# A hybrid decoder layer on one core: the gates of the recurrence made in two groups of two chunks

## The chip, the cores and the metric

The kernel runs on one core of a Trainium2 chip. The metric is the device time of one execution in microseconds (us). The median of the runs is given, with the lowest and the highest. One further execution was taken with the hardware profiler, and all views below are of that one.

## The reference

One layer for 512 tokens of width 1024: a half-step SwiGLU feed-forward part, a mixer, and a second half-step SwiGLU part, each between two RMS norms. Only the mixer matters here. It projects its input to four things: the recurrence's input (4 chunks of 128 channels), the recurrence's output gate, the queries of 8 heads (again 4 chunks of 128 rows), and the keys and values of 2 heads.

```
def block_diag(x, w, b):                      # 8 blocks of 64 x 64
    xh = x.reshape(bsz, s, LRU_BLOCKS, LRU_BLOCK)
    y = jnp.einsum("bshi,hij->bshj", xh, w).reshape(bsz, s, D_LRU)
    return y + b

def rg_lru(x_in, ...):
    xc = causal_depthwise_conv(x_in, conv_w, conv_b)
    r = sigmoid(block_diag(xc, w_rg, b_rg))
    i = sigmoid(block_diag(xc, w_ig, b_ig))
    log_a = LRU_C * r * log_sigmoid(lam)
    a, mult = exp(log_a), sqrt(-expm1(2.0 * log_a))
    u = mult * (i * xc)
    ...                                       # h[t] = a[t] * h[t-1] + u[t]

def hybrid_mixer(h, ...):
    ...
    y_lru = rg_lru(x_lru, ...) * gelu(gate_lru)
    y_attn = sliding_window_sink_attention(q, k, v, sinks)
    y = concatenate([rms_norm(y_lru, g_lru_out), rms_norm(y_attn, g_attn_out)])
    return y @ w_o
```

Attention runs in blocks of 128 queries over a band of two blocks of keys.

## The kernel before

The activations lie with channels on the partitions and the 512 tokens along the row, so a chunk is a tile of 128 x 512. Every float32 product is made of three matmuls on a high and a low part (`mm3`, L505 to L507): high times high, high times low, low times high. A product of a full chunk has 8 steps of 3, so 24 matmuls.

The order of instructions on each engine is the order of the calls in the source (the schedule is manual). What can still shift is only when each instruction starts: it waits for its operands and, where it is the first to write a tile, for all users of the old tile whose buffer it takes over. Four pools of buffers matter: `bank` gives one of 8 PSUM banks, `t2k` one of 38 SBUF tiles of 2 KB a partition, `wt` one of 8 SBUF working tiles (tag "w"), and `home` is one wide tile that holds the queries and keys for the first block. When the program is built, a new `wt` tile is put in a buffer that an earlier one has given up.

The stretch in question, in the order of the calls:

- `conv(0, xps)` makes the convolution of chunks 0 and 1: ACT starts each (L1443), and DVE adds three taps to each (L1447). `split_xc(ci)` then rounds a chunk to its high part on ACT (`xch`, L1473) and takes the low part on POOL (`xcl`, L1474).
- `in_product("pk")`, `in_product("pv")` and, in the loop over j, `in_product(f"pq{j}")` are the products for keys, values and the four query chunks on TensorE (PE). Each `W.take` in them also splits weights that come later: the high part on ACT (`whi`, L209), the low part on DVE or POOL (`wlo`, L214).
- `conv(2, xps)` makes the convolution of chunks 2 and 3, ahead of the loop.
- In round j of the loop: the query product `pq{j}`; `split_xc(j + 1)`; `lru_gates(j)`; and `in_parts`, which handles the query: DVE scales it into the working tile `qT{j}` (L1427) and copies the first 128 tokens to `home` (L1487), ACT rounds it (L1493), DVE takes the low part (L1494). In round 0 four transposes of the values follow (`vt`, L1513), which DVE copies out (L1515).
- `lru_gates(ci)` makes the two gates of one chunk. The blocks are 64 x 64, and the two halves of the partitions (`SIDE`) are multiplied at the same time in two halves of the array: 3 pairs of matmuls (L1455) into the banks `rg` and `ig`. ACT takes two sigmoids (L1457, L1459). They hold one half of each gate, so two transfers from SP's queue (L1458, L1460) put the halves of the input gate together in the working tile `ig`, POOL multiplies it into the chunk (L1462, written `xc<-ig,xc` in the views), and POOL's queue moves the other half (L1463).
- After the loop ACT loads the table for the exponential (L481), and the attention starts: the first scores `cur` (L1597) need all four query copies in `home`; DVE masks them and takes the maximum (L1616, L1617, L1631), ACT takes the exponentials (L1642), PE transposes them (`pt`, L1652) and ACT copies them out (L1654). Between these PE works at the products of the output gate (`gt`).

Of the kernel before, what the change touches and what calls it, by code (L numbers as in the profile page):

```python
# [11 lines left out]
AF = mybir.ActivationFunctionType  # L12
# [11 lines left out]
KC = C // P  # L24
# [97 lines left out]
def tile_layer(ctx: ExitStack, tc: tile.TileContext, out: bass.AP, **ins: bass.AP):  # L122
    nc = tc.nc
    pe, dve, act, pool, sync = nc.tensor, nc.vector, nc.scalar, nc.gpsimd, nc.sync
# [14 lines left out]
    SIDE = [slice(0, HD), slice(HD, P)]  # L139

    def bank(name):
        return psum.tile([P, T], F32, tag="bank", name=name)

    def t2k(name, dt=F32):
        return big.tile([P, T], dt, tag="t2k", name=name, bufs=NT2K)
# [3 lines left out]
    def fours(name, dt):  # L149
        t = big.tile([P, NB * T], dt, tag="z", name=name, bufs=2)  # L150
        return [t[:, i * T:(i + 1) * T] for i in range(NB)]
# [10 lines left out]
    def wt(name, w=T, dt=F32):  # L162
        return tmp.tile([P, w], dt, tag="w", name=name, bufs=NW)
# [5 lines left out]
    def load_raw(srcs, nk, w, name):  # L169
        raw = wpool.tile([P, nk * w], F32, tag="raw", name=f"raw_{name}", bufs=NRAW).rearrange("p (k c) -> p k c", k=nk)  # L170
        o = 0
        for src in srcs:
            n = src.shape[1]
            sync.dma_start(raw[:, :, o:o + n], src.rearrange("(k p) c -> p k c", p=P))
            o += n
        return raw
# [215 lines left out]
    for g, (f0, f1) in enumerate(GROUPS2):  # L392
        if g == 0:
            for f in range(f0, f1, 2):
                add_gate_up(w2, f, "b")
            r = W.raw(lambda f=f0: load_raw([ins["ffn2_w_down"][0, f * P:(f + 2) * P, :]], 2, D, f"bd{f}"))
# [40 lines left out]
    for i in range(2):  # L437
        load_x(0, i)
        for o in (0, F):
            r = first_raw[o, i] = t2k(f"first{o}{i}").rearrange("p (k c) -> p k c", k=4)  # L440
# [9 lines left out]
    for name, n in ROWS:  # L450
        if name in ("b_rg", "b_ig"):

            j = name == "b_ig"
# [33 lines left out]
    def colrange(name):  # L487
        lo, n = col_of[name]
        return cols[:, lo:lo + n]

    def col(name, i):
        return colrange(name)[:, i:i + 1]
# [16 lines left out]
    def product(w, xs, sl=ALL, name="", hooks=()):  # L509
        ps = bank(name)  # L510
        hooks = dict(hooks)
        for k, x in enumerate(xs):
            if k in hooks:
                hooks[k]()
            mm3(ps[:, sl], w, k, [t[:, sl] for t in x], k == 0, k == len(xs) - 1)
        return ps
# [683 lines left out]
    banks = [bank(f"a_first{i}") for i in range(4)]  # L1200
# [96 lines left out]
    gw, home = {}, []  # L1297
# [125 lines left out]
    def in_product(name, hooks=(), ahead=AHEAD):  # L1423
        return product(W.take(ahead), mx.xs, name=name, hooks=hooks)

    def scaled(t, b):
        dve.tensor_mul(t, b, R)  # L1427
        return t

    xcs, th, rs_, us_ = [], [], [], []  # L1430
# [15 lines left out]
                ci = c0 + j  # L1446
                dve.scalar_tensor_tensor(xcs[ci], xps[ci][:, 1 + w:1 + w + T], col("conv_w", w * KC + ci), xcs[ci], op0=ALU.mult, op1=ALU.add)  # L1447

    def lru_gates(ci):

        banks = bank(f"rg{ci}"), bank(f"ig{ci}")
        (hi, lo), (xh, xl) = gw["both"], xc_parts[ci]
        for i, (w, x) in enumerate(((hi, xh), (hi, xl), (lo, xh))):
            for ps, half in zip(banks, SIDE):
                pe.matmul(ps, w[half, ci, :], x[half, :], start=i == 0, stop=i == 2)  # L1455
        r, other, ig = t2k(f"r{ci}"), wt(f"other{ci}"), wt(f"ig{ci}")
        act.activation(r, banks[0], AF.Sigmoid, bias=col("b_rg", ci))  # L1457
        sync.dma_start(ig[SIDE[0], :], r[SIDE[1], :])  # L1458
        act.activation(other, banks[1], AF.Sigmoid, bias=col("b_ig", ci))  # L1459
        sync.dma_start(ig[SIDE[1], :], other[SIDE[0], :])  # L1460
        u = xcs[ci]
        pool.tensor_mul(u, ig, u)  # L1462
        pool.dma_start(r[SIDE[1], :], other[SIDE[1], :])  # L1463
        t = t2k(f"th{ci}")
        rs_.append(r)
        us_.append(u)
        th.append(t)

    xc_parts = {}

    def split_xc(ci):
        xh, xl = wt(f"xch{ci}", T, F32R), wt(f"xcl{ci}", T, F32R)
        act.copy(xh, xcs[ci])  # L1473
        pool.tensor_sub(xl, xcs[ci], xh.bitcast(F32))  # L1474
        xc_parts[ci] = xh, xl
# [8 lines left out]
    def in_parts(b, first, name, low=dve):  # L1484

        x = scaled(wt(name), b)
        dve.tensor_copy(first, x[:, :P])  # L1487
        if name == "qT3":
            spare.extend(fours("attn", F32R))
            xh, xl = spare.pop(), spare.pop()  # L1490
        else:
            xh, xl = t2k(f"{name}h", F32R), t2k(f"{name}l", F32R)
        act.copy(xh, x)  # L1493
        low.tensor_sub(xl, x, xh.bitcast(F32))  # L1494
        return xh, xl

    conv(0, xps)
    split_xc(0)
    kT = in_parts(pk, k0, "kT", pool)
    pv = in_product("pv")  # L1500
    vT = scaled(wt("vT"), pv)
    conv(2, xps)
    qT = []
    for j in range(4):
        b = in_product(f"pq{j}")
        if j < KC - 1:
            split_xc(j + 1)
        lru_gates(j)
        qT.append(in_parts(b, q0[:, j * P:(j + 1) * P], f"qT{j}", deferred if j == 3 else dve))
        if j == 0:  # L1510
            vt = bank("vt")
            for b in range(NB):
                pe.transpose(vt[:, b * P:(b + 1) * P], vT[:, b * P:(b + 1) * P], ident)  # L1513
            v = home[0][:, P + 2 * T:P + 2 * T + 8 * (HD + 1)]
            dve.tensor_copy(v.rearrange("p (h d) -> p h d", d=HD + 1)[:, :, :HD], vt.rearrange("p (h d) -> p h d", d=HD))  # L1515
# [285 lines left out]
    ws, banks = [], []  # L1801
# [31 lines left out]
    banks = boundary(res, late, ysp, None, n2, "m")  # L1833
# [192 lines left out]
```

## Time and profile before

| | us |
|---|---|
| median of 3 runs | 844.31 |
| lowest, highest | 844.1, 844.48 |
| the profiled execution | 844.61 |
| its span, first to last instruction | 842.9 |
| PE busy in the span | 834.0 (99%) |
| DVE busy | 729.9 (87%) |
| ACT busy | 520.7 (62%) |
| POOL busy | 184.6 (22%) |

The profiled execution took 1.7 us more than its span, and 0.3 us more than the median. A busy PE is only one that has a matmul under way; matmuls overlap, and how tightly they follow each other is read from their starts. In the views a row of the timeline gives start, duration, engine, line, operation, tiles (out<-in) and count, and in brackets how long the engine had stood idle before it and what ended that. Buffer numbers are left out, so the four queries are all called `qT` and the four chunks `xc`.

### The profile page before, as it was taken

The numbers are of one execution on the slowest core, as the hardware profiler recorded it, in microseconds if no ns is written. First come the engines' busy times: TensorE is split into PE (matmuls) and PEld (weight loads), VectorE is DVE, ScalarE is ACT, GpSimd is POOL, SyncE is SP. The second block draws the span as 40 slices with busy tenths as digits, with TensorE's granted clock in tenths as the row PEclk, the third lists the DMA queues.
The fourth block names the chain that finished last, engine by engine and source line by source line (L and its number), as shares of the span: only waits on it lengthen the run. The fifth ranks groups of instructions, "written<-read, shape, count | busy, mean of one in ns | idle before, by whom it ended". The sixth has DMA issues, their size and how long they took to land.

```text
span 842.9 us, 12574 instructions
## 1 busy us (share of the span) xinstructions
PE 834.0 (99%) x4568; PEld 722.1 (86%) x4568; DVE 729.9 (87%) x1031; ACT 520.7 (62%) x837; POOL 184.6 (22%) x197
## 2 busy tenths in 40 slices
PE   9999999999999999999999999999999999999997
PEld 8988888988988998997788899888888888888886
DVE  4978999998979865889789589799998998998996
ACT  6746856666666654456796456436657767666562
POOL 2023000140320333334521055112004114032001
PEclk9999999999999999999999999999999999999999
DMA  7249419397595799222511131169539939769742
GB/s 251 77 132 350 155 54 323 81 247 257 131 248 184 170 268 335 77 80 90 157 51 51 50 107 45 51 127 276 192 105 230 316 96 250 256 147 254 304 145 101
DMA packets 123614, 143.74 MB, mean 171 GB/s; under 512 B 23896, under 2 KB 81568, under 8 KB 123040
## 3 DMA queue, kind: packets, MB, share of 16 engines
q1 hardware_dynamic: 109232, 111.86, 41.6%
q0 software_dynamic: 14176, 30.94, 17.0%
q8 instruction: 36, 0.59, 0.3%
q14 instruction: 26, 0.21, 0.1%
q10 hardware_dynamic: 144, 0.13, 0.0%
HBM read 100.45 MB, written 40.89 MB: 168 GB/s over the span
## 4 chain that ended last, share of the span: by engine, by line
PE 93%; DVE 3%; ACT 2%; DMA 1%; issue 0%; POOL 0%; DVEq 0%; POOLq 0%; ACTq 0%
PE ab L955 10%; PE aa L955 10%; PE da L955 5%; PE db L955 5%; PE yaa L1346 3%; PE bb L955 3%; PE ba L955 3%; PE yda L1346 2%; PE ya L505 2%; PE ya L506 2%; PE ya L507 2%; PE a_first L1205 1%; PE aa L885 1%; PE yab L1867 1%; PE yab L1866 1%; PE yab L1865 1%
## 5 line engine op out<-in xcount | busy, mean ns | idle before, releaser
L1115 POOL DMA_DIRECT2D yp_a<-stage x42 | 36.8, 1065 | 181.0 <-ACT stage L1112 163.5
L1115 POOL DMA_DIRECT2D yp_b<-stage x42 | 36.3, 1053 | 144.0 <-ACT stage L1112 121.4
L505 PE MATMUL ya<-hha,whi_ad 128*128 128x512 f32 x62 | 24.1, 389 | 0.0
L506 PE MATMUL ya<-hla,whi_ad 128*128 128x512 f32 x62 | 24.1, 389 | 0.0
L507 PE MATMUL ya<-hha,wlo_ad 128*128 128x512 f32 x62 | 24.1, 389 | 0.0
L688 POOL TENSOR_TENSOR acca_r<-acca_r,sq_r 128x512 f32<-128x512 f32 x6 | 8.1, 1357 | 63.7 <-ACT sq_r L536 63.7
L1984 POOL TENSOR_TENSOR last<-yp,grow 128x512 f32<-128x512 f32 x3 | 3.9, 1293 | 58.3 <-DVE yp L1974 58.3
L524 PE MATMUL an<-xh_mx,whi_xl 128*128 128x256 f32 x64 | 15.8, 287 | 0.0
L525 PE MATMUL an<-xh_mx,wlo_xl 128*128 128x256 f32 x64 | 15.5, 283 | 0.0
L1981 ACT ACTIVATE ysq<-yp 128x512 f32<-128x512 f32 (+1 forms) x8 | 4.9, 607 | 15.9 <-DVE yp L1974 15.9
L505 PE MATMUL gt<-xh_mx,whi_gt 128*128 128x512 f32 x32 | 14.2, 444 | 0.0
L507 PEld LDWEIGHTS ya<-hha,wlo_ad 128*128 128x128 f32 x62 | 11.6, 188 | 2.4
L505 PEld LDWEIGHTS ya<-hha,whi_ad 128*128 128x128 f32 x62 | 11.6, 188 | 2.4
L506 PEld LDWEIGHTS ya<-hla,whi_ad 128*128 128x128 f32 x62 | 11.6, 188 | 2.4
L1112 ACT COPY stage<-yab 128x512 f32<-128x512 f32 x12 | 6.5, 604 | 11.3 <-DMA yp_b<-stage 11.3
L505 PE MATMUL pq<-xh_mx,whi_q 128*128 128x512 f32 x32 | 12.8, 400 | 0.0
L536 ACT ACTIVATE sq_r<-yp_a 128x256 f32<-128x256 f32 (+1 forms) x10 | 5.0, 502 | 12.3 <-DVE yp_a L678 5.9
L505 PE MATMUL pub<-xh_f,whi_bu 128*128 128x512 f32 x32 | 12.6, 395 | 0.0
L507 PE MATMUL gt<-xh_mx,wlo_gt 128*128 128x512 f32 x32 | 12.6, 394 | 0.0
L505 PE MATMUL pgb<-xh_f,whi_bg 128*128 128x512 f32 x32 | 12.6, 393 | 0.0
L506 PE MATMUL gt<-xl_mx,whi_gt 128*128 128x512 f32 x32 | 12.5, 392 | 0.0
L506 PE MATMUL pq<-xl_mx,whi_q 128*128 128x512 f32 x32 | 12.5, 390 | 0.0
(2017 smaller groups left out, 3501.7 us busy)
## 6 DMA issues: line engine op xcount, KB each, us to landing
yp_a<-stage POOLq DMA_DIRECT2D x50, 256.0 KB, 8.8
yp_b<-stage POOLq DMA_DIRECT2D x50, 256.0 KB, 9.1
h_a<-za SPq DMA_DIRECT2D x16, 256.0 KB
hxa<-h_a SPq DMA_DIRECT2D x16, 256.0 KB
h_b<-zb SPq DMA_DIRECT2D x16, 256.0 KB
hxb<-h_b SPq DMA_DIRECT2D x16, 256.0 KB
xn<-in_x SPq DMA_DIRECT2D x8, 256.0 KB
xT_hbm<-xT POOLq DMA_DIRECT2D x2, 1024.0 KB, 9.3
```

The costliest lines, as they stand in the source:

```text
L505: pe.matmul(ps, hi[:, k, :], xh, start=start, stop=False)
L506: pe.matmul(ps, hi[:, k, :], xl, start=False, stop=False)
L507: pe.matmul(ps, lo[:, k, :], xh, start=False, stop=stop)
L524: pe.matmul(ps[:, sl], hi[:, k, :], xh, start=k == 0, stop=False)
L525: pe.matmul(ps[:, sl], lo[:, k, :], xh, start=False, stop=False)
L885: pe.matmul(o, w[:, k, js], x, start=first and i + j + k == 0, stop=k == 3 and i == 2, skip_group_check=True)
L955: pe.matmul(b[tb], x[:, blk], w[:, k, :], start=first and q + k + j == 0, stop=q + k == 2 and j == 2, skip_group_check=True)
L1115: pool.dma_start(o, st.rearrange("p (a b) -> p a b", a=2) if len(o.shape) == 3 else st, accum_op=ALU.add)
L1205: pe.matmul(banks[j][:, HALF[0]], ws[j][part][:, k, :], n1.xs[k][xpart][:, HALF[0]], start=k == 0 and part == xpart, stop=stop and k == KD ...
L1346: pe.matmul(o, a[:, k, ms], x[:, js], start=first and i + k + m % 2 == 0, stop=k == 1 and i == 2, skip_group_check=True)
L1865: pe.matmul(banks[i], hh[:, js], hi[:, k, :], start=first and k == 0, stop=False, skip_group_check=True)
L1866: pe.matmul(banks[i], hh[:, js], lo[:, k, :], start=False, stop=False, skip_group_check=True)
```

## The change

`lru_gates` now takes a tuple of chunks and a function to be called between its two parts. First it issues the matmuls of all its chunks, step by step over the three parts and within a step chunk by chunk; then the sigmoids and SP's transfers of all its chunks; then `between()`; and then POOL's products and transfers. It is called twice: behind query product 0 for chunks 0 and 1, and behind query product 2 for chunks 2 and 3. No gates stand behind products 1 and 3 any more. Chunk 1 is split ahead of the value product; chunks 2 and 3 are split in `between()` of the first group, that is, on ACT behind four sigmoids and on POOL ahead of the first two products `xc<-ig,xc`. The number of instructions of each kind is unchanged.

```
-    def lru_gates(ci):
-        banks = bank(f"rg{ci}"), bank(f"ig{ci}")
-        (hi, lo), (xh, xl) = gw["both"], xc_parts[ci]
-        for i, (w, x) in enumerate(((hi, xh), (hi, xl), (lo, xh))):
-            for ps, half in zip(banks, SIDE):
-                pe.matmul(ps, w[half, ci, :], x[half, :], start=i == 0, stop=i == 2)
...
+    def lru_gates(cs, between=lambda: None):
+        banks = {ci: (bank(f"rg{ci}"), bank(f"ig{ci}")) for ci in cs}
+        hi, lo = gw["both"]
+        for i in range(3):
+            for ci in cs:
+                xh, xl = xc_parts[ci]
+                w, x = ((hi, xh), (hi, xl), (lo, xh))[i]
+                for ps, half in zip(banks[ci], SIDE):
+                    pe.matmul(ps, w[half, ci, :], x[half, :], start=i == 0, stop=i == 2)
+        gates = {}
+        for ci in cs:
+            r, other, ig = gates[ci] = t2k(f"r{ci}"), wt(f"other{ci}"), wt(f"ig{ci}")
+            act.activation(r, banks[ci][0], AF.Sigmoid, bias=col("b_rg", ci))
+            sync.dma_start(ig[SIDE[0], :], r[SIDE[1], :])
+            act.activation(other, banks[ci][1], AF.Sigmoid, bias=col("b_ig", ci))
+            sync.dma_start(ig[SIDE[1], :], other[SIDE[0], :])
+        between()
+        for ci in cs:
+            r, other, ig = gates[ci]
+            u = xcs[ci]
+            pool.tensor_mul(u, ig, u)
+            pool.dma_start(r[SIDE[1], :], other[SIDE[1], :])
...
     kT = in_parts(pk, k0, "kT", pool)
+    split_xc(1)
     pv = in_product("pv")
...
         b = in_product(f"pq{j}")
-        if j < KC - 1:
-            split_xc(j + 1)
-        lru_gates(j)
+        if j == 0:
+            lru_gates((0, 1), lambda: (split_xc(2), split_xc(3)))
+        if j == 2:
+            lru_gates((2, 3))
         qT.append(in_parts(b, q0[:, j * P:(j + 1) * P], f"qT{j}", deferred if j == 3 else dve))
```

The buffers that the working tiles take over move with it. In the built program of before, the write of `qT0` waits for no product `xc<-ig,xc`, and the write of `qT2` waits for that of chunk 1, whose `ig` buffer it takes. In the built program of after, the write of `qT0` takes the buffer of `ig` of chunk 0 and waits for POOL's product of chunk 0; the write of `qT1` waits for that of chunk 1; the writes of `qT2` and `qT3` wait for none. The bank of query product 3 is that of query product 0 in both.

More of the change, by code (lines that the diff above doesn't have):

```diff
@@ L1447, in conv @@
                 dve.scalar_tensor_tensor(xcs[ci], xps[ci][:, 1 + w:1 + w + T], col("conv_w", w * KC + ci), xcs[ci], op0=ALU.mult, op1=ALU.add)
-    def lru_gates(ci):
-        banks = bank(f"rg{ci}"), bank(f"ig{ci}")
-        (hi, lo), (xh, xl) = gw["both"], xc_parts[ci]
-        for i, (w, x) in enumerate(((hi, xh), (hi, xl), (lo, xh))):
-            for ps, half in zip(banks, SIDE):
[L1455 to L1467, printed above, removed]
+    def lru_gates(cs, between=lambda: None):
[20 more added lines that the diff above has]
+            pool.dma_start(r[SIDE[1], :], other[SIDE[1], :])
+            rs_.append(r)
+            us_.append(u)
+            th.append(t2k(f"th{ci}"))
     xc_parts = {}
```

## The prediction

> **What bounds the kernel now.** I read the page first, then the waits by engine, then the chain that ended last, and then the timelines of the mixer's start, engine by engine.
>
> ```profile
> span 842.9 us, 12574 instructions
> PE 834.0 (99%) x4568; PEld 722.1 (86%) x4568; DVE 729.9 (87%) x1031; ACT 520.7 (62%) x837; POOL 184.6 (22%) x197
> ...
> PE atp L1763 <- DVE yn L1704: 0.6, 1, 0.6
> ...
> 409.23 0.89 PE cur L1597 x16
> ...
> 413.08 0.52 ACT sc L1642 x2
> ...
> 455.88 1.64 PE atp L1763 x13
> ```
>
> TensorE is busy for 99% of the span, and in the mixer it waits once, 0.6 us for DVE at `atp`. From 413 to 456 the chain runs through ACT and DVE instead, and its start is PE's own place: ACT copies out what PE has just transposed. So PE and that chain move together: what delays PE at the first scores, `cur`, comes out at the end whole, and what it gains there comes out too. At most the 0.6 us at `atp` could still give way. The question is when `cur` is done. The rows of PE around it:
>
> ```profile
> 394.85 0.39 PE L507 MATMUL pq<-xh_mx,wlo_q 128*128 128x512 f32 x1
> 395.16 0.50 PE L1455 MATMUL rg<-xch,gates 64*128 64x512 f32 x1
> ...
> 396.05 0.50 PE L505 MATMUL pq<-xh_mx,whi_q 128*128 128x512 f32 x1
> 396.39 0.39 PE L506 MATMUL pq<-xl_mx,whi_q 128*128 128x512 f32 x1
> 396.62 0.40 PE L507 MATMUL pq<-xh_mx,wlo_q 128*128 128x512 f32 x1
> ...
> 407.95 0.39 PE L507 MATMUL pq<-xh_mx,wlo_q 128*128 128x512 f32 x1
> 408.27 0.50 PE L1455 MATMUL rg<-xch,gates 64*128 64x512 f32 x1
> ...
> 409.07 1.05 PE L1597 MATMUL cur<-home 64*128 64x128 f32 x16
> ...
> 413.60 0.60 PE L1652 MATMUL pt<-ident,sc 128*128 128x128 f32 x4
> ```
>
> **The change on PE.** Full matmuls follow each other at 0.23 us (396.39 to 396.62). From the last matmul of product 1 (394.85) to the second of product 2 (396.39) are 1.54 us, where two steps of 0.23 would be 0.46: a group of gates costs 1.08 us. Its three pairs are worth 0.69; the other 0.39 is the change from full rows to half rows and back. Before, there are four such changes (the last group and `cur` share one); after, there are three: two double groups, and `cur` alone. Up to the end of product 3, PE gains 3 pairs (0.69) ahead of product 1, loses a whole group (1.08) ahead of product 2, and gains 0.69 ahead of product 3: its last matmul goes from 407.95 to 408.25. `cur` follows 0.32 later (as 408.27 follows 407.95), at 408.57 instead of 409.07; with the 0.11 us that the first matmul after a change costs, PE by itself is 0.39 us earlier. That is all there is to win there.
>
> `cur` goes through the four query chunks in turn; the fourth starts after three quarters of the chain's 0.89 us, at 409.07 + 0.67 = 409.74 before, and could start at 409.3 after. It needs the copy of `qT3`.
>
> **The change on DVE and POOL.** Here is the price.
>
> ```profile
> 389.11 6.04 DVE L1447 SCALAR_TENSOR_TENSOR xc<-xp,cols,xc 128x512 f32<-128x512 f32 x6 [0.51 <-ACT xc L1443]
> ...
> 396.21 0.68 DVE L1427 TENSOR_TENSOR qT<-pq,R_mx 128x512 f32<-128x512 f32 x1
> ...
> 400.01 0.68 DVE L1427 TENSOR_TENSOR qT<-pq,R_mx 128x512 f32<-128x512 f32 x1
> ...
> 404.39 0.69 DVE L1427 TENSOR_TENSOR qT<-pq,R_mx 128x512 f32<-128x512 f32 x1 [1.18 <-POOL xc L1462]
> 405.11 1.14 DVE L1487 COPY home<-qT 128x128 f32<-128x128 f32 x1
> 406.18 0.68 DVE L1494 TENSOR_TENSOR qT2l<-qT,qT2h 128x512 fp32r<-128x512 f32 x1
> 406.78 1.21 DVE L214 TENSOR_TENSOR wlo_gt<-raw_gt__4100,whi_gt 128x1024 fp32r<-128x1024 f32 x1
> 408.38 0.69 DVE L1427 TENSOR_TENSOR qT<-pq,R_mx 128x512 f32<-128x512 f32 x1 [0.39 <-PE pq L507]
> 409.11 0.23 DVE L1487 COPY home<-qT 128x128 f32<-128x128 f32 x1
> ```
>
> ```profile
> 396.38 1.29 POOL L1462 TENSOR_TENSOR xc<-ig,xc 128x512 f32<-128x512 f32 x1 [3.77 <-DMA ig<-other]
> 397.61 0.56 POOL L1463 DMA_DIRECT2D r<-other  x1
> ...
> 404.86 1.30 POOL L1474 TENSOR_TENSOR xcl<-xc,xch 128x512 fp32r<-128x512 f32 x1
> 406.86 2.28 POOL L1462 TENSOR_TENSOR xc<-ig,xc 128x512 f32<-128x512 f32 x1 [0.70 <-DMA ig<-other]
> ```
>
> ```profile
> 392.55 0.69 ACT L1457 ACTIVATE r<-rg,cols 128x512 f32<-128x512 f32 x1
> 393.14 0.68 ACT L1459 ACTIVATE other<-ig,cols 128x512 f32<-128x512 f32 x1
> ...
> 400.73 0.62 ACT L1493 CAST qT1h<-qT 128x512 fp32r<-128x512 f32 x1 [0.55 <-DVE qT L1427]
> 401.25 1.05 ACT L209 CAST whi_gt<-raw_gt__4100 128x1024 fp32r<-128x1024 f32 x1
> ...
> 411.06 1.28 ACT L481 ACT_TABLE_LOAD   x1
> ...
> 412.47 1.13 ACT L1642 ACTIVATE sc<-cur,nm 128x128 f32<-128x128 f32 x4
> 414.28 0.59 ACT L1654 COPY pa<-pt 128x512 f32<-128x512 f32 x1 [0.68 <-issue]
> ```
>
> Two things show. First, DVE and POOL hold each other up when both work from SBUF alone: the copy at 405.11 takes 1.14 us and ends with POOL's split (404.86 + 1.30), while its twin at 409.11 takes 0.23; POOL's product at 406.86 takes 2.28 instead of 1.29 and ends 1.15 us after DVE's weight split (406.78 + 1.21). Reading a query from PSUM (408.38) is not held. Second, a query may wait for a buffer: at 404.39 DVE waited 1.18 us for POOL's product of chunk 1.
>
> After, `qT0` is the one that waits, for POOL's product of chunk 0, and that product now stands behind both splits of chunks 2 and 3, which need the second convolution:
>
> - The convolution ends at 395.15 now (389.11 + 6.04). ACT's rounding of chunk 1 (0.62) goes ahead of the weights, which delays what follows on ACT and DVE by up to 0.6; POOL's split of chunk 1 no longer falls into the convolution, which saves up to 1.0 of waiting. I take 395.45, between 394.9 and 396.0.
> - ACT rounds both chunks behind four sigmoids, which end at 395.0 (from 392.55, 0.59 apart): chunk 2 at 395.6, chunk 3 at 396.2. By then DVE has started a weight split (1.21) at the end of the convolution, to 396.6. POOL then does two splits and the product, 3 x 1.29 less small overlaps: 400.3. If POOL gets in ahead of DVE, the same four pieces fill the same time.
> - So `qT0` starts at 400.35 instead of 396.21, and everything behind it on DVE's queue with it: the rest of query 0, the copy of `vt`, a weight split, `qT1`.
> - Round 0 took 3.80 (396.21 to 400.01). Its copy to `home` now meets POOL's second product: 400.3 + 0.56 of issuing + 1.29 = 402.1, 0.3 later in the round than the first product's end was. `qT1` at 404.4. Its own buffer is free by then.
> - Round 1 took 3.20 without its wait (400.01 to 404.39 less 1.18): `qT2` at 407.55.
>
> ACT holds round 2:
>
> - ACT rounds `qT1` 0.72 after its start (400.01, 400.73), at 405.1; the weights' high part from 405.65 to 406.7; then four sigmoids in a row at 0.59 (392.55, 393.14), to 409.0; then it rounds `qT2`, to 409.6. PE has filled their banks by 403, but in ACT's queue they stand behind `qT1`.
> - DVE's low part of `qT2` starts at 409.6; from there to the next query are 1.73 (406.18 to the end of 406.78 + 1.21, less 0.08 of overlap): `qT3` at 411.35, its copy from 412.07.
> - POOL's product of chunk 2 comes 2.56 us after the sigmoid that ends at 407.9 (393.14 + 0.68 to 396.38), at 410.45, waits for the weight split and runs from 411.35 to 412.65. The copy ends with it, at 412.7.
>
> The fourth quarter of `cur` starts at 412.75 instead of 409.74: **+3.0 us**. Product 3 takes the bank of product 0, which DVE has read by 401.0, and PE reaches it 23 steps ahead of 408.25, at 403: no wait.
>
> The sum's ends: with the convolution at 394.9 and no turn lost to POOL at the last copy (0.4), +2.0; with POOL's products of chunks 2 and 3 both ahead of DVE's last weight split and copy (another 1.29 less 0.1), +4.2. The 0.6 us at `atp` would lower the first end to +1.4 if it went, which I don't expect: the exponentials of the first block come at 414.8 (the table, 1.28, is loaded by 414.0), are done by 415.95, and PE reaches the transposes at 413.60 + 3.0 = 416.6. So from there all is as before, 3.0 later.
>
> On SP's queue the second load of the output weights stood between gate transfers and now stands behind all of them, at about 409.6.
>
> ```profile
> 404.62 0.54 SPq L174 DMA_DIRECT2D raw_wo__4325<-in_w_o  x1
> ...
> 427.01 1.03 ACT L209 CAST whi_wo<-raw_wo__4325 128x1024 fp32r<-128x1024 f32 x1
> ```
>
> Its first reader comes 22.4 us after its issue, which leaves more than 17: nothing. The sigmoids of chunk 3 are earlier than before, and their readers are not waiting.
>
> The profiled execution took 844.61 us for 842.9 of span; I expect 847.6 and 845.9, and 844.31 + 3.0 = 847.3 for the median. A change of 0.2% is 1.7 us, about what a measurement of this kernel can tell from none.
>
> **The rivals.**
>
> *POOL and DVE run freely (845.7).* If they don't exclude each other and the stretched rows have another cause, the convolution and the copies are quicker. `qT0` then waits only for ACT and POOL: chunk 2 rounded at 395.6, two splits and a product, 399.5. Without held copies round 0 takes 3.7 and round 1 3.1, so `qT1` comes at 403.2; ACT's row of work behind it (0.7 + 0.5 + 0.95 + 4 x 0.59 + 0.62) puts the low part of `qT2` at 408.4, `qT3` at 410.1 and its copy at 411.1: +1.4, or +0.8 if the wait at `atp` goes. That is not slower by what can be measured. It decides at a last copy by 411.4. For it: DVE stood idle at two queries above, 1.57 us together. Against it: 1.14 and 0.23 for the same copy, and POOL's 2.28. A last copy by 409.7, which would be no loss at all, would need `qT0` by 398, and the four sigmoids and two splits ahead of it don't allow that. Chance 0.10.
>
> *POOL takes the turns (848.5).* POOL's products for chunks 2 and 3 fall just where `qT3` is scaled and copied; if they win, +4.2. For it: at 406.86 POOL stood only 0.08 behind DVE. Chance 0.15.
>
> *The clock falls (849.0).* PE stands still from about 409.3 to 412.75, 3.4 us in one piece.
>
> ```profile
> 382.00:410.00 28.00, 28.00 (x144) 21.51 (x142) 24.30 (x30) 18.34 (x26) 16.87 (x12) 1.00 0.38 113
> ```
>
> Here PE never rested (28.00 busy of 28.00 us) at a granted clock of 1.00, so no row shows what a rest does. If matmuls ran at twice their pitch of 0.23 for as long again, half of 3.4 would be lost: +3.0 + 1.7. [...] Chance 0.07.
>
> **How the numbers follow.** The forecast has 0.66: 0.63 from +1.7 to +3.6, and 0.03 under that. POOL's turns have 0.15, the clock 0.07, the free run 0.10, and 0.02 stay for a gain by waits that I don't see. Slower is 0.63 + 0.15 + 0.07 = 0.85, same 0.03 + 0.10 = 0.13, faster 0.02. The range goes from 845.6 (+1.3), just under the free run, to 848.9 (+4.6), the end of the clock's case; outside lie the 0.02 and about half of the free run, of the short end and of the clock, 0.12 in all. Leaving out the free run whole would leave out 0.2, but its bound hangs on ACT's row, which is the surest of the terms, so I keep it in.
>
> **What would show it.** In the profile of after: DVE's first `qT` at about 400 instead of 396.2 with POOL's `xc` as its releaser; POOL with two splits and two products in a row from 396; ACT with four sigmoids in a row from about 406.6, ahead of the rounding of `qT2`; the fourth `qT` after 411; a wait of PE at `cur` for DVE's copy `home`, 3 us or more, where none was; and from `pt` on the rows of before, 3 us later, with 0.6 left at `atp`. The prediction is wrong if `qT0` comes before 399, if PE doesn't wait at `cur`, or if that wait is made good before `atp`.

## The result, and the profile after

| | us |
|---|---|
| before, median of 6 runs | 844.17 (843.98 to 844.48) |
| after, median of 6 runs | 849.85 (848.6 to 851.09) |
| ratio, with its 95% interval | 1.0062 (1.0052 to 1.0073) |
| the profiled execution of after | 850.22, span 848.5 |

The kernel is 5.7 us slower. The forecast was 847.3 us, with a range up to 848.9: the direction was right, the size was not. The changed kernel was run five times more, beside the experiments: 849.04 us (848.33 to 850.58) against 844.33, ratio 1.006 (1.0048 to 1.0073).

First the waits of TensorE (total, times, longest):

```profile
PE cur L1606 <- DVE home L1494: 3.0, 1, 3.0
...
PE atp L1772 <- DVE yn L1713: 0.6, 1, 0.6
```

The wait at `cur` is new; the 0.6 us at `atp` is as before. The timelines of DVE, POOL and ACT in the stretch that the prediction went through:

```profile
400.49 0.69 DVE L1427 TENSOR_TENSOR qT<-pq,R_mx 128x512 f32<-128x512 f32 x1 [3.67 <-POOL xc L1470]
...
404.63 0.68 DVE L1427 TENSOR_TENSOR qT<-pq,R_mx 128x512 f32<-128x512 f32 x1
...
407.73 0.69 DVE L1427 TENSOR_TENSOR qT<-pq,R_mx 128x512 f32<-128x512 f32 x1
...
409.76 0.69 DVE L1501 TENSOR_TENSOR qT2l<-qT,qT2h 128x512 fp32r<-128x512 f32 x1 [1.08 <-ACT qT2h L1500]
...
411.51 0.68 DVE L1427 TENSOR_TENSOR qT<-pq,R_mx 128x512 f32<-128x512 f32 x1
412.23 0.57 DVE L1494 COPY home<-qT 128x128 f32<-128x128 f32 x1
```

```profile
395.81 3.40 POOL L1481 TENSOR_TENSOR xcl<-xc,xch 128x512 fp32r<-128x512 f32 x2 [3.99 <-ACT xch L1480]
399.18 1.28 POOL L1470 TENSOR_TENSOR xc<-ig,xc 128x512 f32<-128x512 f32 x1
...
410.62 2.11 POOL L1470 TENSOR_TENSOR xc<-ig,xc 128x512 f32<-128x512 f32 x1 [7.87 <-DMA ig<-other]
```

```profile
406.81 0.68 ACT L1462 ACTIVATE r<-rg,cols 128x512 f32<-128x512 f32 x1
...
409.10 0.63 ACT L1500 CAST qT2h<-qT 128x512 fp32r<-128x512 f32 x1
```

Both holds are there: the first query waits 3.67 us for POOL's product behind two splits, and the rounding of `qT2` stands behind four sigmoids. Now TensorE:

```profile
408.65 0.39 PE L507 MATMUL pq<-xh_mx,wlo_q 128*128 128x512 f32 x1
408.97 0.94 PE L1606 MATMUL cur<-home 64*128 64x128 f32 x12
412.86 0.80 PE L1606 MATMUL cur<-home 64*128 64x128 f32 x4 [2.95 <-DVE home L1494]
...
414.60 0.63 PE L507 MATMUL gt<-xh_mx,wlo_gt 128*128 128x512 f32 x1
415.03 0.63 PE L505 MATMUL gt<-xh_mx,whi_gt 128*128 128x512 f32 x1
...
419.58 0.60 PE L1661 MATMUL pt<-ident,sc 128*128 128x128 f32 x4
```

The full matmuls of the output gate follow each other at 0.43 us (414.60 to 415.03), not at 0.23. From the fourth quarter of `cur` to `pt` it takes 6.72 us; before, it took 3.86 (409.74 to 413.60). So 2.86 us were lost behind the wait, with the matmuls at the longer pitch. Counted from `kT`, whose start is a mark ahead of the change (384.17 and 384.43), `pt` is 5.72 us late. The table by stretches (PE busy is the first pair of columns after the length, PEclk the granted clock), cut at 412.08 and 418.91, where the clock changed, and in steps of 3.41 us, half the time between them:

```profile
408.67:412.08 3.41, 1.23 (x14) 0.75 (x12) 2.33 (x4) 2.01 (x3) 1.47 (x1) 1.00 0.86 190
412.08:415.49 3.41, 2.63 (x9) 2.02 (x10) 2.46 (x4) 2.10 (x3) 2.87 (x4) 0.50 0.99 302
415.49:418.91 3.42, 3.42 (x10) 2.65 (x9) 3.28 (x8) 1.14 (x4) 0.00 (x0) 0.50 1.07 323
418.91:422.32 3.41, 3.41 (x35) 2.81 (x33) 1.00 (x3) 2.04 (x7) 0.63 (x1) 1.00 0.13 33
```

The granted clock was 0.50 from 412.08, while TensorE still stood idle, until 418.91: 6.83 us, two stretches of 3.41. What the stage cost as a whole is read between two marks outside it, the scaling of `kT` and the first transpose of `atp`. Before, then after (durations, then first and last start):

```profile
L1427 DVE TENSOR_TENSOR kT<-pk,R_mx x1: 681/681/681, 384.2 to 384.2; 128x512 f32<-128x512 f32 x1
...
L1763 PE MATMUL atp<-ident,home x8: 270/272/328, 454.6 to 457.0; 128*128 128x128 f32 x8
```

```profile
L1427 DVE TENSOR_TENSOR kT<-pk,R_mx x1: 683/683/683, 384.4 to 384.4; 128x512 f32<-128x512 f32 x1
...
L1772 PE MATMUL atp<-ident,home x8: 270/273/328, 460.2 to 462.6; 128*128 128x128 f32 x8
```

That is 70.4 us before and 75.8 after: 5.4 of the 5.6 us between the two profiled executions lie in this stage, and about 0.36 of the 5.72 us at `pt` is made good ahead of `atp`.

### The profile page after: what moved, and what is told of

Its sections match the earlier page's. It is cut to its first block, busy times and chain, and to the rows that moved or that the text cites. A ratio compares the mean times of both kernels' runs of the same rounds, so it can differ in the third digit from the quotient of the medians.

```text
span 848.5 us, 12569 instructions
## 1 busy us (share of the span) xinstructions
PE 836.3 (99%) x4568; PEld 724.0 (85%) x4568; DVE 729.3 (86%) x1031; ACT 520.9 (61%) x837; POOL 183.8 (22%) x197
## 4 chain that ended last, share of the span: by engine, by line
PE 94%; DVE 3%; ACT 1%; DMA 1%; issue 0%; POOL 0%; SPq 0%; DVEq 0%; ACTq 0%; POOLq 0%
PE ab L955 10%; PE aa L955 10%; PE da L955 5%; PE db L955 5%; PE yaa L1346 3%; PE bb L955 3%; PE ba L955 3%; PE yda L1346 2%; PE ya L506 2%; PE ya L505 2%; PE ya L507 2%; PE aa L885 1%; PE a_first L1205 1%; PE yab L1874 1%; PE yab L1876 1%; PE yab L1875 1%
## 5 line engine op out<-in xcount | busy, mean ns | idle before, releaser
L507 PE MATMUL pq<-xh_mx,wlo_q 128*128 128x512 f32 x32 | 12.5, 390 | 0.0
```

Of the source, the lines that this page charges most:

```text
L507: pe.matmul(ps, lo[:, k, :], xh, start=False, stop=stop)
```

## The experiments

The theory: the wait of 3.0 us comes from DVE's queue as predicted, and the rest from the clock, which falls because TensorE idles. The rivals: the sigmoids alone hold the chain; the clock follows something else; later stages cost more.

In the table, the extra time is against the old kernel's median measured beside it; the stage is the length between the two marks above, less 70.4; the wait is TensorE's at the fourth quarter of `cur`; the last column is the time at half clock in the stage. The last three are of one profiled execution each.

| kernel | extra time | stage | wait | half clock |
|---|---|---|---|---|
| after | 5.7 | 5.4 | 2.95 | 6.8 |
| after, again | 4.7 | 4.2 | 3.0 | 3.4 |
| fill13 | 4.9 | 2.9 | none | 0 |
| fill13, again | 4.8 | 2.9 | none | 0 |
| prodfirst | 4.9 | 3.3 | 3.0 | 0 |
| parts_q2 | 3.6 | 3.1 | 1.9 | 3.4 |
| own | 1.0 | 0.9 | 1.1 | 0 |
| own_q2 | 0.6 | 0.1 | 0.2 | 0 |
| first_own | 0.1 | -0.2 | none | 0 |
| late2 | 1.1 | 1.1 | 0.9 | 0 |
| late4 | 4.1 | 3.7 | 2.4 | 3.4 |
| late9 | 8.3 | 8.5 | 6.0 | 6.8 |
| late9_fill | 6.6 | 5.9 | none | 0 |

**Work for TensorE in the wait (fill13).**

```
-                for n in range(2):
-                    pr = slice(n * HD, (n + 1) * HD)
-                    pe.matmul(... q0[pr, j * P:(j + 1) * P], ...)
+                for i in range(14 if j == 3 else 1):
+                    jq = j if j < 3 or i == 13 else 2
+                    for n in range(2):
+                        pr = slice(n * HD, (n + 1) * HD)
+                        pe.matmul(... q0[pr, jq * P:(jq + 1) * P], ...)
```

> The changed kernel, with the score products of chunk 2 repeated 13 times into chunk 3's columns ahead of the fourth quarter of `cur` (which then overwrites them; the result is the same). The quarter still waits for the same copy, so the stall of about 3.0 us stays, but TensorE works through two thirds of it: 12 products took 0.94 us, so 26 take about 2.0. Theory A (stall of 3.0 and then a clock that falls because TensorE idled): the idle time shrinks from 2.95 to about 0.9, the granted clock stays at 1.0 behind it, `pt` comes about 3 us after the old kernel's and not 6, the time is about 847.2 us (+3.0). Rival B (the clock follows the transfers or the time of the stage, or the further 2.7 us are lost elsewhere): the gate products behind the quarter run at half clock all the same, 849.8 us.

Measured: 849.25 us, ratio 1.0058 (1.0044 to 1.0071). TensorE's timeline:

```profile
409.52 4.39 PE L1608 MATMUL cur<-home 64*128 64x128 f32 x68
...
414.87 0.39 PE L506 MATMUL gt<-xl_mx,whi_gt 128*128 128x512 f32 x1
415.10 0.39 PE L507 MATMUL gt<-xh_mx,wlo_gt 128*128 128x512 f32 x1
...
417.37 0.83 PE L1663 MATMUL pt<-ident,sc 128*128 128x128 f32 x4
```

The pitch stays at 0.23 and `pt`, counted from `kT`, is 2.8 us earlier than in the changed kernel, though the copy is as late: the stage costs 2.9, not 5.4. In the stage theory A holds. The time, though, is 2 us above its 847.2, so it was run again.

> The changed kernel with the 13 repeats, once more, to read a second profile of it: in the first, `pt` was 2.86 us later than in the old kernel (offset ahead of the stage taken off), while the time was 4.85 us longer. Theory A (the other 2.0 us are waits of later stages for transfers that land now earlier, now later, by the run): the stage again costs 2.8 to 3.0 us, the offsets ahead of the stage and in the second feed-forward differ from the first profile's (0.83 and 0.95 us there), and the time lies between 847.5 and 849.3. Rival B (the changed kernel costs these 2.0 us in a later stage each time): the same offsets at the same places, 849.3.

Measured: 849.15 us (849.05 to 849.24). The stage is 2.9 again, and the misfit of 2 us too. Half of it has a place: in the second feed-forward part TensorE waits for ACT at two products `ab`. The old kernel's waits, then those of fill13's second profile:

```profile
PE ab L955 <- ACT bb L960: 0.3, 1, 0.3
```

```profile
PE ab L955 <- ACT bb L960: 0.6, 1, 0.6
...
PE ab L955 <- ACT stage L1891: 0.2, 1, 0.2
```

In both profiles of fill13 TensorE falls back by another 0.9 us there against the old kernel; so far rival B is right. In the profile of after it has no such wait and comes 0.4 nearer to the old kernel, so 1.3 of the 2.5 us that fill13 saves in the stage are lost here again. What makes ACT late is open: DVE's split `wlo_bd` waits 1.0 us longer for ACT than in the old kernel (1.7, 0.7), but prodfirst has the longer wait at `ab` (0.6) with 0.8 there. Of the rest, 0.83 and 0.39 us lie in the two profiles ahead of `kT`, where the programs do not differ, as theory A has it, and some 0.4 behind the last matmul. Measured beside it, the changed kernel without the repeats took 849.04 us (after_b, below): keeping the clock shortened the stage and not the time of this kernel. For the clock, the pair below is cleaner.

**The same with an old kernel made late (late9, late9_fill).** The delay is nine more scalings of `qT3`, which write the same values again:

```
         x = scaled(wt(name), b)
+        if name == "qT3":
+            for _ in range(9):
+                scaled(x, b)
```

late9_fill adds the repeats of fill13 to it, 27 of them.

> The old kernel, with the scaling of qT3 done nine times more: TensorE idle for about 9 x 0.6 - 0.35 = 5.05 us. Theory A: the clock is halved for two stretches of 3.4 us, part of them inside the idle time itself: 849.4 for the wait and 1.7 to 2.9 for the clock, 851.1 to 852.3 us in all runs. Rival B: no fall, 849.4. Rival C: over 850.5 with the clock at 1.0.

> The old kernel with the nine extra scalings of qT3, and the score products of chunk 2 repeated 27 times into chunk 3's columns ahead of the fourth quarter of `cur` (overwritten by it). One repeat took 0.21 us (4 products at 0.105 us a pair), so 27 take 5.7 of the 6.0 us that TensorE stood idle. Theory A (the clock falls because TensorE idles): the clock stays at 1.0, the stage costs the wait alone, about 6.0 to 6.3 us, and `pt` comes 2.2 us earlier than without the repeats: 850.7 us (850.4 to 851.3) instead of 852.9. Rival B (the fall comes with the lateness of the stage or the transfers under way): the clock is halved as without the repeats, 852.9.

Measured: late9 852.88 us, ratio 1.0101 (1.0087 to 1.0115); late9_fill 850.89, ratio 1.0077 (1.0064 to 1.009). The wait was 6.0 us and not 5.05, which puts late9 0.6 above its range; the fill's is met. The copy is as late in both (416.08 and 416.24), and the extra time is 1.7 us less where TensorE works (8.3 against 6.6). late9 has two stretches at half clock in the stage, late9_fill none: the clock follows the idleness, and not the lateness. By stretches, first late9:

```profile
408.65:412.06 3.41, 1.70 (x19) 1.31 (x18) 3.09 (x5) 1.27 (x2) 1.46 (x2) 1.00 0.67 198
412.06:415.48 3.42, 0.00 (x0) 0.00 (x0) 3.25 (x6) 0.00 (x0) 1.74 (x2) 1.00 0.92 287
415.48:418.89 3.41, 2.52 (x8) 2.00 (x9) 2.42 (x6) 2.10 (x3) 0.00 (x0) 0.50 0.33 107
```

And late9_fill:

```profile
412.52:415.94 3.42, 3.42 (x67) 3.42 (x66) 3.25 (x6) 0.00 (x0) 1.76 (x2) 1.00 0.92 282
415.94:419.35 3.41, 3.41 (x27) 2.70 (x24) 2.73 (x7) 2.54 (x5) 0.00 (x0) 1.00 0.28 98
```

In late9, behind a stretch with 1.70 us of work the clock stayed; behind one with none it fell; and 2.52 us of work at half clock did not bring it back: the next stretch was at 0.50 too.

**Smaller doses (late2, late4).** `range(2)` and `range(4)` in place of `range(9)`.

> The old kernel, with the scaling of qT3 done two times more, 0.6 us each, so that the copy for the fourth quarter of `cur` comes later and nothing else changes. TensorE then stands idle in front of it for about 2 x 0.6 - 0.35 = 0.85 us. Theory A (each us of the wait costs one us, and the clock falls only behind a longer wait): 844.4 + 0.85 = 845.2 us, clock 1.0. Rival B (any wait here draws a fall of the clock): 847 or more. Rival C (a delay of this stage costs more than itself further on, one or two us in later stages): 846 to 847 with the clock at 1.0.

> The old kernel, with the scaling of qT3 done four times more: TensorE idle for about 4 x 0.6 - 0.35 = 2.05 us. Theory A: 846.5 us while the clock stays, and about 1.3 to 1.7 more (847.8 to 848.2) in the runs in which it falls for one stretch of 3.4 us; the kernel with an idle time of 1.9 us had its clock down for 3.4 us. Rival B (the clock falls by the transfers under way or by the grouping's own work, and not by the idle time): no fall, 846.5 in all runs. Rival C: about 848 with the clock at 1.0.

Measured: late2 845.68 us, ratio 1.0014 (1.0005 to 1.0023), all eleven runs at a clock of 0.998 or 0.999: the wait of 0.9 costs about itself (1.1). late4 848.66, ratio 1.0049 (1.0036 to 1.0063), all five at 0.996 or 0.997: the wait of 2.4 and one stretch at half clock. Theory A both times, with each about 0.5 above its forecast; rivals B and C fall.

**The buffer (own).**

```
-        x = scaled(wt(name), b)
+        x = scaled(tmp.tile([P, T], F32, tag="acc", name=name, bufs=3) if name in ("qT0", "qT1") else wt(name), b)
```

> The changed kernel, with `qT0` and `qT1` written into buffers that were free long before (those of the sums of squares) instead of the buffers of `ig0` and `ig1`; the order of all instructions is the same. Theory A (the whole loss begins at VectorE's wait of 3.67 us for POOL's product): qT0 goes right behind the weights' low part at about 396.8 us, qT1 at about 401, ScalarE's four sigmoids leave by about 406.3, qT3 follows the last query product at about 409.1, the quarter of `cur` waits 0.4 us or less, the clock stays: 843.8 us, that is the old time less the 0.39 us of the saved changes of array form. Rival B (the four sigmoids ahead of the rounding of qT2, by themselves, hold the chain): the rounding stays at 409.1, the low part at 409.7, the quarter is as late as before and the time stays at 849.8. Between them, by how much the sigmoids move up.

Measured: 845.38 us, ratio 1.0013 (1.0004 to 1.0022). DVE and POOL:

```profile
397.24 0.68 DVE L1427 TENSOR_TENSOR qT<-pq,R_mx 128x512 f32<-128x512 f32 x1
...
409.64 0.69 DVE L1427 TENSOR_TENSOR qT<-pq,R_mx 128x512 f32<-128x512 f32 x1 [0.22 <-PE pq L507]
410.36 1.04 DVE L1494 COPY home<-qT 128x128 f32<-128x128 f32 x1
```

```profile
410.06 1.25 POOL L1470 TENSOR_TENSOR xc<-ig,xc 128x512 f32<-128x512 f32 x1 [5.90 <-DMA ig<-other]
```

The loss goes from 5.7 to 1.0 us with one buffer rule changed and not one instruction moved. The four sigmoids still stand ahead of `qT2`'s rounding, but earlier, and `qT3` waits only for TensorE. What is left is POOL's product of chunk 2, which now falls on the copy: 1.04 us instead of 0.23, until 411.4. Theory A in the mechanism, but 1.6 us above its 843.8: 0.8 is that product, which it had not seen, and the rest is not placed.

**The order on ACT (parts_q2).** `in_parts` for `qT2` is called between the second group's matmuls and its sigmoids.

```
-    def lru_gates(cs, between=lambda: None):
+    def lru_gates(cs, between=lambda: None, parts=lambda: None):
...
+        parts()
         gates = {}
...
         if j == 2:
-            lru_gates((2, 3))
+            lru_gates((2, 3), parts=parts)
-        qT.append(in_parts(b, q0[:, j * P:(j + 1) * P], f"qT{j}", ...))
+        if j not in (2,):
+            parts()
```

> The changed kernel, with the scaling, copy, rounding and low part of qT2 queued ahead of the second group's four sigmoids, transfers and products, on ScalarE and VectorE; the matmuls' order is the same, and qT0 waits for POOL as in the changed kernel. Theory A: qT2 stays at 407.7, its rounding comes at 408.45 instead of 409.10, its low part at 409.1 instead of 409.76, qT3 at 410.8, its copy at 411.5 and no longer held by POOL's product (0.23 us instead of 0.57): the quarter waits about 2.0 us instead of 2.95, that is 846.2 us without a fall of the clock and about 849 with one. Rival B (the sigmoids hold the chain alone): the wait vanishes, 843.8. Whether the clock still falls after 2.0 us of idle tells where its point lies.

Measured: 848.01 us, ratio 1.0045 (1.0032 to 1.0058). A wait of 1.9 us, copy at 412.08 taking 0.23, and in the profiled run one stretch at half clock: theory A, 1 us under its 849 (four of five runs at a clock of 0.996, one at 0.999 and 847.34 us). The sigmoids' place is worth 1 us of the 3. By stretches:

```profile
410.41:413.82 3.41, 1.46 (x9) 1.16 (x9) 2.76 (x5) 3.39 (x6) 0.58 (x1) 1.00 0.66 151
413.82:417.23 3.41, 3.41 (x10) 2.63 (x9) 3.34 (x5) 2.14 (x6) 3.13 (x4) 0.50 0.92 295
```

TensorE worked 1.46 us of the first, and the next was at half clock.

**Both (own_q2).** The edits of own and of parts_q2 together.

> The changed kernel with both edits: `qT0` and `qT1` in buffers of their own, and qT2's scaling, copy, rounding and low part queued ahead of the second group's four sigmoids. With the first alone the quarter still waited 1.1 us, because its copy of 128x128 took 1.04 us beside POOL's product of chunk 2 at 410.06. Theory A (what is left of the loss is that product, brought forward by the grouping into the copy's way): with the sigmoids behind the rounding the product comes about 2.3 us later, at about 412.3, the copy takes 0.23 us, the quarter waits 0.3 us or less, and the time is 844.1 us (843.7 to 844.6), so the saved changes of form (0.39 us) come to light. Rival B (the two saved changes of form are worth nothing in the end, or VectorE's masking behind the copy is now held by the product): 845.0 to 845.4, as with the first edit alone.

Measured: 845.19 us, ratio 1.001 (1.0001 to 1.0019). The copy is free, and the next step is held in its place:

```profile
409.84 0.23 DVE L1495 COPY home<-qT 128x128 f32<-128x128 f32 x1
410.64 1.32 DVE L1629 COPY_PREDICATED cur<-up,home 128x512 f32<-128x512 uint8 x1 [0.58 <-PE cur L1610]
```

The product runs from 410.14, not from 412.3: it waits for its transfers, and the sigmoids' move by 1.7 us (404.63 to 406.34) did not move it. The masking takes 1.32 instead of 0.70. The time is rival B's, but its cause is not shown: the stage is only 0.1 longer than in the old kernel, so the held masking is made good by `atp`. Counted from `kT`, `cur` starts 0.39 us earlier than in the old kernel and its fourth quarter 0.06 later, so here the saved changes of form are used up by the wait for the copy; in the profile another 0.3 us are lost at `ab` in the second feed-forward part.

**POOL's products ahead of the splits (prodfirst).**

```
-        between()
         for ci in cs:
             r, other, ig = gates[ci]
...
             th.append(t2k(f"th{ci}"))
+        between()
```

> The changed kernel, with the splits of chunks 2 and 3 (ScalarE's rounding, POOL's low part) behind POOL's two products `xc<-ig,xc` and not ahead of them. Theory A: the products leave POOL by about 397.8 us, qT0 follows at once, about 2.6 us earlier than in the changed kernel, the quarter of `cur` waits 0.5 us or less and the clock stays; the second group's matmuls then wait little for the splits (low part of chunk 3 at about 402, second group due at about 401.5): 844.3 us (843.8 to 845.0). Rival B (VectorE's wait is made by POOL's load and not by the order): the splits and the products just change places and the time stays near 849.8.

Measured: 849.32 us, ratio 1.0063 (1.005 to 1.0075): as slow as the changed kernel. DVE, then POOL:

```profile
397.92 0.69 DVE L1427 TENSOR_TENSOR qT<-pq,R_mx 128x512 f32<-128x512 f32 x1 [1.19 <-POOL xc L1469]
398.64 4.18 DVE L1494 COPY home<-qT 128x128 f32<-128x128 f32 x1
```

```profile
398.39 1.30 POOL L1469 TENSOR_TENSOR xc<-ig,xc 128x512 f32<-128x512 f32 x1
399.64 0.54 POOL L1470 DMA_DIRECT2D r<-other  x1
400.20 2.53 POOL L1481 TENSOR_TENSOR xcl<-xc,xch 128x512 fp32r<-128x512 f32 x2
```

`qT0` came at 397.9 as expected, and then its copy of 128x128 ended only at 402.82, with POOL's second product and both splits (402.73). The buffer is one way in which POOL holds DVE; this copy, 4.18 us beside POOL and 0.23 alone, is the other. Taking away the first by order only met the second. The expectation missed that.

This run also shows the same wait without a fall, by stretches:

```profile
408.37:411.78 3.41, 1.91 (x17) 1.29 (x15) 2.29 (x4) 2.76 (x5) 0.77 (x1) 1.00 0.70 156
411.78:415.19 3.41, 1.88 (x10) 1.54 (x11) 2.80 (x4) 2.10 (x3) 3.40 (x4) 1.00 0.98 308
```

The wait is 3.0 us as in after, and the clock stays at 1.00. No fall marks the cuts here: where they stand is the author's estimate, and by it the idle time lies half on each side, beside 1.91 and 1.88 us of work.

**The changed kernel again (after_b).**

> The changed kernel itself once more, beside the kernel with the repeats on the same chip. Theory A (3.0 of stall and 2.4 of clock in the stage): `pt` again 5.4 us later than in the old kernel where the clock falls for two stretches, about 4.3 where it falls for one, 3.0 to 3.4 where it stays; 849.9 us (848.4 to 851.1). Rival B (the clock's fall is worth little in the time, since later waits give it back): the time of the runs with a fall differs from that of the kernel with repeats by 0.6 us or less.

Measured: 849.04 us; the profiled run has one stretch at half clock and a stage of 4.2, as theory A has it. The eleven runs of after and after_b, by mean granted clock: two at 0.999 took 848.33 and 848.6 us; four at 0.995 or 0.996 took 848.7 to 849.47; five at 0.994 took 850.22 to 851.09. So the fall is worth 0.6 us on average in one stretch and 2.1 in two, and the kernel's spread of 2.8 us is mostly this. Against fill13_b's 849.15, the two runs of after_b with one fall (848.97, 849.04) are no slower, which is rival B; the two with two falls are 1.4 slower.

**One group only (first_own).** The edit of own, and:

```
-        if j == 2:
-            lru_gates((2, 3))
+        if j >= 2:
+            lru_gates((j,))
```

> The changed kernel with the first group only: chunks 0 and 1 together behind the first query product, chunk 2 behind the third and chunk 3 behind the fourth as in the old kernel, and `qT0` and `qT1` in buffers of their own. It saves one of the changes of array form, 0.39 us. Theory A (the loss comes from POOL's products and splits standing in VectorE's way, and the last gates' 1.08 us behind the fourth query product are the cover of its scaling and copy): VectorE is free, chunk 2's product runs at about 408.0 to 409.3 and holds the copy of 128x128 until 409.4 at most, still ahead of TensorE at about 410.0, so no wait at `cur` and 844.2 us (843.9 to 844.6) beside 844.5 for the old kernel. Rival B (the copy or the masking is held as with both groups): 845.2 to 845.5.

Measured: 844.39 us, ratio 1.0 (0.9991 to 1.0009).

```profile
408.83 0.31 DVE L1494 COPY home<-qT 128x128 f32<-128x128 f32 x1
```

No wait at `cur`, and a stage 0.2 us shorter, but no gain that the time shows. It is the best of the variants, and not better than the old kernel.

## Why the prediction was wrong, and where it was right

- **TensorE alone, -0.39:** right in the rows. `cur` starts at 408.97 against 409.07, and the profile of after is 0.26 us late already at `kT` (384.43 against 384.17): -0.36.
- **`qT0` at 400.35 by its buffer:** 400.49, with the releaser named. own shows that this wait is the root of most of the loss, 4.7 of 5.7 us.
- **`qT1` 404.4, `qT2` 407.55, low part 409.6, `qT3` 411.35, copy done at 412.7, fourth quarter 412.75:** measured 404.63, 407.73, 409.76, 411.51, 412.8 and 412.86. With the 0.26 taken off, the quarter is 2.86 us late where +3.0 was predicted. fill13 confirms the +3.0 in the stage: 2.9.
- **"From `pt` on as before, 3.0 later", and the clock at a chance of 0.07:** here the prediction failed. The 0.07 was the author's estimate; no row of before showed what a rest does to the clock. In the runs a rest did not have to fill a stretch of 3.41 us: one with 1.46 us of work (parts_q2) was followed by a fall, one with 1.70 (late9) was not. Nor did a rest of about 3 us always bring a fall: prodfirst's profiled run, with 3.0, had none in the stage, and 3 of the 16 runs of after and prodfirst kept a mean clock of 0.999, where the other 13 had 0.994 to 0.996. What decides between the two is not shown. The likeliest case was the stall and the clock.
- **The clock's price, +1.7:** mis-sized, on a term that varies. It supposed 3.4 us at twice the pitch, as long as a rest of 3.4 us, which no row of before showed. In after the pitch went from 0.23 us to 0.43 and the rest was 2.95 (the first three quarters of `cur` run until 409.91, not 409.3); the half clock lasted none, 3.4 or 6.8 us by the run, worth 0.6 or 2.1 us in time (1.7 in late9 against late9_fill). In the profiled run it was 2.86 at `pt`.
- **The rest:** even the runs without a fall were at 848.3 to 848.6, inside the range but over 4 us above the old kernel, where the forecast gives 3. About 1 us of that is not traced; no profile of such a run of the changed kernel was taken. fill13 has a like excess, half of it at `ab` in the second feed-forward part, from a cause that stays open.
- **The rivals:** POOL and DVE running freely is refuted by prodfirst's copy of 4.18 us. POOL taking the turns did not come: its product of chunk 2 was done at 412.73, that of chunk 3 stood behind the copy.

## What to carry to other kernels

Ahead of grouping work on one engine, follow which buffers its side products hold, and who takes them over: here a rotation of eight buffers put a query behind another engine's queue, and a buffer of its own took away five sixths of the loss. A wait of two or three microseconds on TensorE is not to be priced at its length: in these profiles 1.46 us of work or less in a stretch of 3.41 at the full clock was followed by one or two stretches at half clock, 1.70 or more by none. The last small group behind the last big product was the cover for that product's way through DVE: even with DVE freed (own_q2), the 0.39 us saved in array changes went into the wait that the cover had hidden.

## What was not expected of the hardware

- The clock fell inside a rest, 2.2 us after TensorE had stopped (after, 409.91 to 412.08) or 5.1 (late9, 410.36 to 415.48), and not at its end. In after a stretch at half clock with 2.63 us of work (412.08 to 415.49) was followed by another at half clock, and one with 3.42 us (415.49 to 418.91) by the full clock.
- A copy that takes 0.23 us alone (before, 409.11) took 4.18 beside POOL (prodfirst, 398.64 to 402.82), across the end of one POOL instruction (399.69), 0.54 us in which POOL only issued a transfer, and two more instructions (until 402.73).
- Scaling from PSUM (0.68 us; after, 411.51) and maxima (0.69; own_q2, 412.00) kept their times beside POOL's products, while the masking went from 0.70 (before, 410.16) to 1.32 (own_q2) and 1.37 (after).
